# The first product of one MLP by seven block products in place of eight, in a two-layer fp32 transformer kernel on one core

## The chip, the core and the metric

The kernel runs on one core of one Trainium2 chip. The metric is the device time of one execution in microseconds. A core has TensorE (PE, matrix products into the eight banks of PSUM), VectorE (DVE), ScalarE (ACT), GpSimd (POOL) and SyncE (SP), which issues the DMAs. Each engine works through its own instructions in order.

## The reference

Two layers over 512 latent and 256 context tokens of 1024 features, all in fp32. Layer 0 mixes by neighbourhood attention, layer 1 by sliding-window attention; each mixer is followed by an MLP with 4096 hidden features. Cut to what matters here (layer 0, both token streams):

```python
h_lat = h_lat + ga1 * (mixer(u_lat) @ wo);  h_ctx = h_ctx + cga1 * (mixer(u_ctx) @ wo)
u = modulate(rms_norm(h, g_mlp), shift, scale)      # h * (1 + scale) + shift
h = h + ga2 * (jnp.square(jax.nn.relu(u @ w1)) @ w2)   # w1: 1024 x 4096, w2: 4096 x 1024
```

Shifts, scales and gates come from `ada_w`, 1024 x 6144 for each layer, times a conditioning vector for the latent and one for the context tokens ("ada").

## The kernel before

Features lie on the 128 partitions: `hT` has eight tiles of 128 features (`KT = 8`), with the 512 latent and the 256 context tokens (`L`, `C`, `T = 768`) in the free dimension. To keep fp32 precision every operand is split in two parts of type fp32r, x = H + L (`split`: a copy on ScalarE rounds to H, a subtraction on GpSimd or VectorE gives L), and a product is three matmuls: wH·uH + wH·uL + wL·uH.

The order of work isn't that of the source. `_build` records steps (engine, operands) in a `Plan`; `Plan.search` then runs a list scheduler with costs of its own over them, many times with shaken ranks, keeps the best order found up to each `mark()`, and writes each engine's queue in that order. Steps made with `gv` may go to GpSimd or VectorE, with `sv` to ScalarE or VectorE, as the planner finds best; `squared` to ScalarE or VectorE.

**Wo.** After attention, `Wo` makes eight feature tiles `f` for the latent tokens (24 matmuls of 512 columns each) and eight for the context tokens (24 of 256). Its weights come in two halves of four units (each one DMA of 128 x 1024 and one split): `take(0)` covers f = 0..3 and puts the first unit into `wx`, the others into `wslots[2]`, `[0]`, `[3]`; `early` starts three tiles while the last head pair's attention runs; `rest` does what is left, adds to `hT` with VectorE, and `Stats` sums the squares.

**The MLP of layer 0** (`mlp(0, True, ...)`). u is made by `modulate`: for each f a multiply-add on VectorE, an activation on ScalarE for uH, another multiply-add for uL. Then come 16 chunks of 256 hidden features (two blocks j of 128). `mlp1` makes the first product of a chunk: for each j and each of the eight k three matmuls for 512 latent columns and three for 256 context columns, 96 in all; `relu2` takes the square of the relu and splits it into `hH`, `hL` (a ring of four). `mlp2` makes the second product: for each of the eight f six matmuls of 512 and six of 256 columns, and after each group VectorE adds the scaled sum to `hT`:

```python
v.scalar_tensor_tensor(out=h, in0=ps, scalar=mods[layer][:, 5, f, col : col + 1], in1=h, op0=ALU.mult, op1=ALU.add)
```

The first product uses PSUM banks 4 and 5 (latent), 0 and 1 (context), the second 2 and 3 (latent), 6 and 7 (context). The weights of w1 and w2 come through `Stream`, four units of 128 x 1024 ahead, into eight slots. Between the products the generator `ada` for layer 1 runs piece by piece: for each of 6 kinds and 8 k a 128 x 1024 tile of `ada_w` is multiplied by two columns of the conditioning vector (ScalarE, or GpSimd for one of them where k is odd) and added into two accumulators (VectorE or GpSimd).

**Layer 1's start.** `kv1` normalizes the latent tokens (`modulate` reads `hT`), stores `hT` to `h_d`, and projects keys and values; `roped` multiplies them by tables in `rope`. Mask and `rope` lie in the columns of `FA` that held the context part of `hT`; they are filled before `kv1` (GpSimd memset and select, a DMA of `rope`, four GpSimd products).

Of the kernel before, what the change touches and what calls it, by code (L numbers as in the profile page):

```python
# [11 lines left out]
F32 = mybir.dt.float32  # L12
R32 = mybir.dt.float32r
# [538 lines left out]

LAST = 3
# [7 lines left out]
def _build(nc, tc, a, es):  # L561
# [145 lines left out]
    hT_lat = FA[:, 0:4096].rearrange("p (f n) -> p f n", f=KT)  # L707
    hT_ctx = FA[:, 4096:6144].rearrange("p (f n) -> p f n", f=KT)
# [8 lines left out]
    def mm(ps, st, mv, start, stop):  # L717
        pe.matmul(ps, st, mv, start=start, stop=stop)
# [17 lines left out]
    def ada(layer, kinds, ring, acc, tmp, ps, depth):  # L736
# [3 lines left out]
        jobs = [(kind, k) for kind in kinds for k in range(KT)]  # L740
        w = {}

        def fetch(i):
            if i < len(jobs):
                kind, k = jobs[i]
                w[i] = ring.next(1024)
                load(w[i], a["ada_w"][layer, k * 128 : (k + 1) * 128, kind * D : (kind + 1) * D])
# [12 lines left out]
        for i in range(depth):  # L760
            fetch(i)
        for i, (kind, k) in enumerate(jobs):
            x = w.pop(i)
            if k == 0:
                (g.tensor_scalar(out=acc[0], in0=x, scalar1=s32[:, k, 0:1], scalar2=None, op0=ALU.mult) if k % 2 else s.activation(acc[0], x, AF.Copy, scale=s32[:, k, 0:1]))
                s.activation(acc[1], x, AF.Copy, scale=s32[:, k, 1:2])
            else:
                (g.tensor_scalar(out=tmp, in0=x, scalar1=s32[:, k, 0:1], scalar2=None, op0=ALU.mult) if k % 2 else s.activation(tmp, x, AF.Copy, scale=s32[:, k, 0:1]))
                gv.tensor_tensor(out=acc[0], in0=acc[0], in1=tmp, op=ALU.add)
                s.activation(x, x, AF.Copy, scale=s32[:, k, 1:2])  # L770
                gv.tensor_tensor(out=acc[1], in0=acc[1], in1=x, op=ALU.add)
            if k < KT - 1:
                fetch(i + depth)
                yield
# [5 lines left out]
            row = x[:, 0:512]  # L780
            s.copy(row, ps)
            yield
            finish(kind, row)
            fetch(i + depth)
# [53 lines left out]
    class Stream:  # L838
# [14 lines left out]
        def next(self, fill=True):  # L853
            self.fill(1)
            u = self.items[self.i][1]
            self.i += 1
            if fill:
                self.fill(self.ahead)
            return u[:, 0:1024], u[:, 1024:2048]

# [369 lines left out]

    class Wo:
# [86 lines left out]
    wo0 = Wo(0, True, lambda ctx, f: (hT_ctx if ctx else hT_lat)[:, f])  # L1318
# [99 lines left out]
    ad = ada_pe(0, (2, 3, 4, 5), Ring(FA, 2048, 1024, 2), lambda kind: banks[5], 2)  # L1418
# [12 lines left out]
    wo0.take(0, Stream(Ring(FA, FX, 1024, 2), [(a["wo0"][0, q], u) for q, u in enumerate((wx, wslots[2], wslots[0], wslots[3]))], 4))  # L1431
# [11 lines left out]
    def mlp(layer, T_ctx, stream, tmp, side, st_lat, st_ctx, between=None, after_ctx=None):  # L1443
        if T_ctx:
            p1, p1c, p2, p2c = Banks(4, 5), Banks(0, 1), Banks(2, 3), Banks(6, 7)
        else:
            p1, p1c, p2, p2c = Banks(4, 5, 0, 1), Banks(0), Banks(2, 3, 6, 7), None
        nt = T if T_ctx else L
        hr = Ring(RA, RW + 14336, 1536, 4)
        def relu2(ps, n, hH, hL):  # L1450
# [7 lines left out]
        def mlp1(c, between=None):  # L1458
# [3 lines left out]
            def start(j, fill=True):  # L1462
                W[j] = stream.next(fill)
                u = hr.next()
                hs.append((u[:, 0:nt], u[:, 768 : 768 + nt]))

            def part(pss, js, uH, uL, hook=None, lo=0):
                hi = lo + pss[0].shape[1]
                for k in range(KT):
                    if hook and k == 4:  # L1470
                        hook()
                    sl = slice(k * 128, k * 128 + 128)
                    for ps, j in zip(pss, js):
                        wH, wL = W[j]
                        mm(ps, wH[:, sl], uH[:, k, lo:hi], k == 0, False)
                        mm(ps, wH[:, sl], uL[:, k, lo:hi], False, False)
                        mm(ps, wL[:, sl], uH[:, k, lo:hi], False, k == KT - 1)

            def lat(*js, hook=None, halves=False):
                pss = [p1.next() for j in js]  # L1480
                if halves:
                    for j in js:
                        part([pss[j][:, 0:256]], [j], uH_lat, uL_lat)
                        if j == 0:
                            hook()
                    part([ps[:, 256:512] for ps in pss], js, uH_lat, uL_lat, lo=256)
                else:
                    part(pss, js, uH_lat, uL_lat, hook)
                for ps, j in zip(pss, js):
                    relu2(ps, 512, hs[j][0][:, 0:512], hs[j][1][:, 0:512])  # L1490

            def ctx(*js):
                if T_ctx:
                    pss = [p1c.next()[:, 0:256] for j in js]
                    part(pss, js, uH_ctx, uL_ctx)
                    for ps, j in zip(pss, js):
                        relu2(ps, 256, hs[j][0][:, 512:768], hs[j][1][:, 512:768])

            if between:
# [3 lines left out]
                if T_ctx:  # L1503
                    lat(0, 1, hook=between)
                else:
                    lat(0, 1, hook=between, halves=True)
                stream.fill(stream.ahead)
                ctx(0, 1)
            else:
                start(0)  # L1510
                lat(0)
                run(side, 1)
                ctx(0)
                run(side, 1)
                start(1)
                lat(1)
                run(side, 1)
                ctx(1)
                run(side, 1)
            return hs  # L1520

        def mlp2(c, hs, last):
            W = [stream.next() for j in range(2)]

            def one(ps, f, lo, hi, hT, col):
                at = col * 512
# [7 lines left out]
                h = hT[:, f, lo - at : hi - at]  # L1534
                v.scalar_tensor_tensor(out=h, in0=ps, scalar=mods[layer][:, 5, f, col : col + 1], in1=h, op0=ALU.mult, op1=ALU.add)

            if last and T_ctx:
                pc = Banks(1, 6, 0)
                for f in range(KT):
                    one(pc.next()[:, 0:256], f, 512, 768, hT_ctx, 1)  # L1540
                    st_ctx.step(hT_ctx[:, f], v if f == KT - 1 else g)
                pl = Banks(2, 3, 4, 5)
                for f in range(KT):
                    one(pl.next(), f, 0, 512, hT_lat, 0)
                    st_lat.step(hT_lat[:, f], v if f == KT - 1 else g)
                    if f == 1:
                        st_ctx.finish()
                        after_ctx()
            elif last:
                for f in range(KT):  # L1550
                    n = 512 if f < KT - 1 else 256
                    for lo in range(0, 512, n):
                        one(p2.next()[:, 0:n], f, lo, lo + n, hT_lat, 0)
                        sy.dma_start(a["out"][:, f, lo : lo + n], hT_lat[:, f, lo : lo + n])
            else:
                for f in range(KT):
                    one(p2.next(), f, 0, 512, hT_lat, 0)
                    if T_ctx:
                        one(p2c.next()[:, 0:256], f, 512, 768, hT_ctx, 1)
# [3 lines left out]
        p1c = Banks(0)  # L1563
        for c in range(NCH):
            now = nxt
            if c == NCH // 2 and T_ctx:
                mark()
            if c + 1 < NCH:
                nxt = mlp1(c + 1)
                if T_ctx or c:  # L1570
                    stream.eng = v
            if c == NCH - 2 and T_ctx:
                run(side)
                p2, p2c = Banks(2, 3, 4, 5), Banks(6, 0, 1)
            mlp2(c, now, c == NCH - 1)

    def mlp_items(layer):

        w1, w2 = ([(a[n][layer, 2 * c], a[n][layer, 2 * c + 1]) for c in range(16)] for n in ("w1", "w2"))
# [10 lines left out]
    def load1(gr):  # L1590
# [3 lines left out]
    RX, RY = region((R32, 2048), (F32, 2048))  # L1594
    wslots.append(RX[:])
    wu = Slots(*(wslots[i] for i in (4, 5, 6, 7, 0, 1, 2, 3)))
    stream = Stream(
        Ring(FA, FX, 1024, 3),
        [(a["wo0"][1, q], wu.next()) for q in range(4)] + [(x, wu.next()) for x in mlp_items(0)]
        + [(a["wkv1"][q], wslots[q]) for q in range(4)] + [(a["wq1"][0, q], wq[q]) for q in range(2)],  # L1600
        4)
    adar = Ring(FA, FX + 3072, 1024, 2)
    tmp = Ring(FA, FX + 5120, 512, 5)
    tmp2 = Ring(FA, FX + 3072, 512, 9)
    Rm = fr(7680, 768)
    R_lat, R_ctx = Rm[:, 0:512], Rm[:, 512:768]
    st = (Stats(R_lat, 512, tmp2, banks[2]), Stats(R_ctx, 256, tmp2, banks[3]))
# [403 lines left out]
```

## Time and profile before

| | |
|---|---|
| median of 3 runs | 1602.92 us (1602.74 to 1604.47) |
| profiled execution | 1604.45 us, of which the span of the profile is 1602.7 us |
| granted TensorE clock, mean | 0.997 |
| busy: PE / DVE / ACT / POOL | 1581.8 / 1116.0 / 761.0 / 235.6 us |
| second products of the first MLP, first add to the last chunk's first add | 496.3 to 985.1 us |
| DMA | 171.17 MB, mean 107 GB/s |

How to read the rows. A row of groups gives engine, operation, tiles out<-in (without buffer numbers: `pq` are PSUM banks, `RA` the fp32r arrays, `FA` the fp32 arrays, `RX`/`RY` appear as `R`), shape, count, then busy time in us, mean ns of one, and the idle time of the engine before them with what ended it. A row of the timeline or of the chain gives start, us, engine and what, with neighbouring instructions of like tiles merged under the shape of the first. A row of a stretch gives its length, then for PE, PEld (weight loads), DVE, ACT and POOL the busy time and the count, then granted clock, DMA share and GB/s. All instructions bear one line number, that of the place where the planned order is written out (L547), so groups are told apart by their tiles and shapes.

### The profile page before, as it was taken

What the parts mean: (1) busy time and instruction counts of PE and PEld (TensorE: products, weight loads), DVE (VectorE), ACT (ScalarE), POOL (GpSimd) and SP (SyncE); (2) the same over time, 40 slices, a digit from 0 to 9 for tenths busy, and PEclk for the clock granted to TensorE, in tenths of its full rate; (3) what the DMA queues carried; (4) which work ended last, traced back from release to release, by engine and by line L of the source; (5) the groups of instructions that cost most, each with busy time, mean ns of one, the idle gap of its engine ahead of it and who ended that gap; (6) DMA issues with size and microseconds to landing.
All of it is one profiled execution on the core that took longest, in us unless ns stands there. A gap on an engine that the chain in (4) does not pass through costs nothing.

```text
span 1602.7 us, 24512 instructions
## 1 busy us (share of the span) xinstructions
PE 1581.8 (99%) x9372; PEld 1336.8 (83%) x9372; DVE 1116.0 (70%) x2193; ACT 761.0 (47%) x1554; POOL 235.6 (15%) x197
## 2 busy tenths in 40 slices
PE   7999999999999999999999999999999999999999
PEld 5888888987888888888888888798877888888887
DVE  4887765676479667677686857898885855556564
ACT  4676665676355233435343423677782523323320
POOL 0101001010013122313141300232100000000000
PEclk9999999999999999999999999999999999999999
DMA  9654443224314233433342321101044323223211
GB/s 348 173 162 121 124 138 108 61 73 143 104 66 159 91 110 115 132 106 119 122 142 93 119 80 66 33 28 59 29 122 162 106 88 98 89 84 116 93 40 53
DMA packets 60309, 171.17 MB, mean 107 GB/s; under 512 B 7296, under 2 KB 17056, under 8 KB 60064
## 3 DMA queue, kind: packets, MB, share of 16 engines
q1 hardware_dynamic: 60192, 169.61, 33.1%
q8 instruction: 73, 1.20, 0.3%
q14 instruction: 44, 0.36, 0.1%
HBM read 165.30 MB, written 7.43 MB: 108 GB/s over the span
## 4 chain that ended last, share of the span: by engine, by line
PE 91%; DVE 4%; DMA 2%; ACT 1%; issue 1%; SPq 0%; POOL 0%; DVEq 0%; ACTq 0%; POOLq 0%
PE pq L547 91%; DVE RA L547 2%; DVE FA L547 1%; DMA R<-inv_d 1%; DMA FA<-in_ada_w_dram 1%; ACT RA L547 0%; ACT FA L547 0%; DMA FA<-in_wqkv_dram 0%; DVE R L547 0%; DMA FA<-in_xT_dram 0%; SPq L547 0%; DVE smalls L547 0%; ACT R L547 0%; DMA FA<-h_d 0%; POOL FA L547 0%
## 5 line engine op out<-in xcount | busy, mean ns | idle before, releaser
L547 PE MATMUL pq<-RA 128*128 128x512 f32 (+3 forms) x6560 | 1282.8, 348 | 5.2 <-DVE RA L547 2.2
L547 PEld LDWEIGHTS pq<-RA 128*128 128x128 f32 x6560 | 1053.6, 189 | 154.8 <-issue 10.5
L547 ACT CAST RA<-FA 128x1024 fp32r<-128x1024 f32 (+3 forms) x283 | 223.8, 811 | 377.9 <-PE pq L547 273.2
L547 DVE SCALAR_TENSOR_TENSOR FA<-pq,mods,FA 128x512 f32<-128x512 f32 (+1 forms) x413 | 261.7, 659 | 166.2 <-PE pq L547 165.0
L547 DVE TENSOR_TENSOR RA<-FA,RA 128x1024 fp32r<-128x1024 f32 (+3 forms) x236 | 242.6, 1038 | 94.2 <-ACT RA L547 89.6
L547 PE MATMUL pq<-RA,R 128*128 128x512 f32 (+1 forms) x870 | 189.9, 351 | 0.1
L547 PEld LDWEIGHTS pq<-RA,R 128*128 128x128 f32 x870 | 145.3, 189 | 24.2 <-issue 0.8
L547 POOL TENSOR_TENSOR RA<-FA,RA 128x512 fp32r<-128x512 f32 (+2 forms) x47 | 77.0, 1639 | 502.0 <-ACT RA L547 461.4
L547 PE MATMUL pq<-ident,FA 128*128 128x128 f32 x800 | 133.2, 274 | 0.9 <-DVE RA L547 0.3
L547 DVE TENSOR_TENSOR R<-R,FA 128x1024 f32<-128x1024 f32 x84 | 109.6, 1331 | 15.0 <-ACT FA L547 8.6
L547 PEld LDWEIGHTS pq<-ident,FA 128*128 128x128 f32 x800 | 96.7, 140 | 17.3 <-issue 2.0
L547 ACT ACTIVATE FA<-FA,smalls 128x512 f32<-128x512 f32 (+1 forms) x120 | 89.0, 742 | 43.3 <-DVE smalls L547 42.6
L547 POOL TENSOR_SCALAR FA<-FA,s 128x1024 f32<-128x1024 f32 x24 | 75.3, 3136 | 197.6 <-DMA FA<-in_ada_w_dram 115.7
L547 ACT ACTIVATE FA<-pq 128x512 f32<-128x512 f32 (+1 forms) x96 | 49.8, 522 | 102.9 <-PE pq L547 99.7
L547 ACT ACTIVATE FA<-FA,s 128x1024 f32<-128x1024 f32 x60 | 69.0, 1151 | 53.7 <-POOL FA L547 43.1
L547 POOL TENSOR_TENSOR FA<-FA 128x256 f32<-128x256 f32 (+2 forms) x51 | 40.5, 800 | 281.4 <-ACT FA L547 143.5
L547 DVE SCALAR_TENSOR_TENSOR FA<-pq,FA 128x512 f32<-128x512 f32 (+1 forms) x96 | 56.7, 595 | 35.9 <-ACT FA L547 35.8
L547 ACT ACTIVATE FA<-FA 128x256 f32<-128x256 f32 (+1 forms) x130 | 58.1, 454 | 47.8 <-DVE FA L547 39.7
L547 POOL TENSOR_TENSOR FA<-FA,smalls 128x128 f32<-128x128 f32 (+2 forms) x54 | 34.5, 640 | 299.7 <-DVE smalls L547 212.3
L547 ACT COPY R<-pq 128x512 f32<-128x512 f32 (+4 forms) x133 | 62.5, 486 | 20.2 <-PE pq L547 19.2
L547 PE MATMUL pq<-R 128*64 128x256 f32 (+3 forms) x432 | 68.4, 456 | 1.9 <-DVE FA L547 1.9
L547 DVE SCALAR_TENSOR_TENSOR RA<-pq,cst,RA 64x128 fp32r<-64x128 f32 (+2 forms) x152 | 57.9, 383 | 14.2 <-ACT RA L547 11.6
(88 smaller groups left out, 912.6 us busy)
## 6 DMA issues: line engine op xcount, KB each, us to landing
FA<-in_w_dram SPq DMA_DIRECT2D x128, 512.0 KB
FA<-in_ada_w_dram SPq DMA_DIRECT2D x80, 512.0 KB
FA<-in_wqkv_dram SPq DMA_DIRECT2D x24, 384.0 KB
FA<-in_wo_dram SPq DMA_DIRECT2D x16, 512.0 KB
FA<-in_ada_dram SPq DMA_DIRECT2D x10, 512.0 KB
FA<-in_wq_dram SPq DMA_DIRECT2D x8, 512.0 KB
R<-inv_d SPq DMA_DIRECT2D x16, 208.0 KB
R<-in_ada_dram SPq DMA_DIRECT2D x6, 512.0 KB
```

Of the source, the lines that this page charges most:

```text
L547: tc.keep_in_program_order(getattr(e, f)(*map(real, args), **{k: real(x) for k, x in kw.items()}))
```

## The change

1. `mlp` is divided: `mlp_one` (layer 1) is what it was, `mlp_zero` (layer 0) is new. The first product is seen as blocks: u is 2 x 2 blocks (k in two halves of `KH = 4` tiles, tokens in two halves of `HT = 384`), a chunk's weights are 2 x 2 blocks too (k halves, j). Chunk 0 (`plain`) makes the eight block products. Chunks 1 to 15 make seven (`head` two, `tail` five), each 4 x 3 matmuls of 384 columns, on sums of weight blocks and of u blocks.
2. The sums of u are made once (`u_first`, `u_rest`, `u_last`), in place in `hT`; so `Wo0` stores h to `hs_d` (16 DMAs) and `u_last` loads it back (8 DMAs). The sums of weights are made for every chunk: four `gv` additions and seven splits of 512 columns, and four splits of w2 quarters (`w20`).
3. In the second product, f = 0, 1, 2 of the latent tokens stay in banks 2, 3, 6 over all chunks; the rest shares banks 5 and 7. The first product uses 4, 0, 1.
4. `ada` works on halves of 512 columns: for k = 0 two ScalarE activations, else two VectorE multiply-adds into the accumulators, with no GpSimd.
5. `Wo0` takes its weights by column quarters: two units (k = 0..3, k = 4..7) serve two f. The order of slots is 2, 0, 3, wx for f = 0..3, and 2, 0, 3, 1 for f = 4..7. `lat_done` (making u) is called before the context tiles f = 4..7.
6. `hT` is one array of 768 columns per f, so mask and `rope` are filled in `kv1` after the stores to `h_d` (`tables`).

```diff
-    def ada(layer, kinds, ring, acc, tmp, ps, depth):
+    def ada(layer, kinds, ring, acc, ps):
...
+            for r in range(2):
+                o = acc[r][:, h * 512 : h * 512 + 512]
+                if k == 0:
+                    s.activation(o, x, AF.Copy, scale=s32[:, k, r : r + 1])
+                else:
+                    v.scalar_tensor_tensor(out=o, in0=x, scalar=s32[:, k, r : r + 1], in1=o, op0=ALU.mult, op1=ALU.add)
...
+    class Wo0:
...
+        def one(self, bk, f, ctx, st):
...
+            v.scalar_tensor_tensor(out=h, in0=ps, scalar=mods[0][:, 2, f, ctx : ctx + 1], in1=h, op0=ALU.mult, op1=ALU.add)
+            st.step(h, v if f == KT - 1 and not ctx else g)
+            sy.dma_start(hs_d[:, f, L:T] if ctx else hs_d[:, f, 0:L], h)
...
+    first = Stream(Ring(FA, FX, 1024, 2), [(a["wo0"][q], u) for q, u in enumerate((wslots[2], wslots[0], wslots[3], wx))], 4)
...
+    def u_of(lo, hi, R, ctx):
+        for f in (0, 4, 1, 5, 2, 6, 3, 7):
+            h = hT[:, f, lo:hi]
+            v.scalar_tensor_tensor(out=h, in0=h, scalar=amod[0][:, 1, f, ctx : ctx + 1], in1=R, op0=ALU.mult, op1=ALU.mult)
+            s.activation(h, h, AF.Identity, bias=mods[0][:, 3, f, ctx : ctx + 1])
+    def u_first():
+        u_of(0, L, R_lat, 0)
+        for f in range(KT):
+            blocks(f, 0, "11" if f < KH else "21")
+    def u_rest(ring):
+        u_of(L, T, R_ctx, 1)
+        for k in range(KH):
+            blocks(k, 1, "12")
+            blocks(k + KH, 1, "22")
+        for k in range(KH):
+            b11, b12, b21, b22 = (hT[:, f, at : at + HT] for f in (k, k + KH) for at in (0, HT))
+            t2 = ring.next(HT)
+            to = lambda name: [x[:, k] for x in UC[name]]
+            v.tensor_tensor(out=b11, in0=b12, in1=b11, op=ALU.subtract)
+            v.tensor_tensor(out=t2, in0=b22, in1=b11, op=ALU.subtract)
+            split(*to("t2"), t2)
+            split(*to("t1"), b11)
+            v.tensor_tensor(out=b12, in0=b22, in1=b12, op=ALU.subtract)
+            split(*to("t3"), b12)
+            v.tensor_tensor(out=b21, in0=b21, in1=t2, op=ALU.subtract)
+    def u_last():
+        for k in range(KH):
+            blocks(k + KH, 0, "t4")
+        for f in range(KT):
+            sy.dma_start(hT[:, f], hs_d[:, f])
+    def mlp_zero(queue, xs, side, st_lat, st_ctx, between, after_ctx):
+        p1, p2 = Banks(4, 0, 1), Banks(5, 7)
+        held = {0: banks[2], 1: banks[3], 2: banks[6]}
...
+            def head(self):
+                self.a, b = self.bk.next()[:, 0:HT], self.bk.next()[:, 0:HT]
+                product(self.a, "11", True, last=False)
+                x = self.kept(self.a)          # sv copy of the bank
+                product(b, "21", True)
+                self.added(0, 0, b, x)         # v add, relu, square, split
...
+            def tail(self):
+                a_, c_ = self.a, self.bk.next()[:, 0:HT]
+                product(a_, "t2", False, last=False)
+                y = self.kept(a_)
+                product(c_, "t1", True, last=False)
+                z = self.kept(c_)
+                product(a_, "t3", False, last=False)
+                self.added(1, 1, a_, z)
+                product(c_, "22", False)
+                self.added(0, 1, c_, y)
+                product(a_, "t4", False)
...
+        pairs = [Pair(Banks(4, 5)), Pair(Banks(0, 1, 2))]
+        queue.ahead = 3
+        W = [queue.next(False) for i in range(4)]
+        pairs[0].plain(W, 0)
+        between()                              # u_rest
+        pairs[1].head()
+        pairs[0].plain(W, 1)
+        queue.ahead = AHEAD                    # 5
+        u_last()
+        pairs[1].tail()
+        for c in range(NCH):
...
+            if 0 < c < NCH - 1:
+                x = Pair()
+                x.head()
+                run(side, 2)
+                x.tail()
+                run(side, 2)
+                pairs.append(x)
...
+            second(pairs[c].h, c == 0, c == NCH - 1)
...
-    g.memset(mask, 0.0)
...
+    def tables():
+        g.memset(mask, 0.0)
...
         for f in range(KT):
             sy.dma_start(h_d[:, f], hT_lat[:, f])
+        tables()
```

More of the change, by code (lines that the diff above doesn't have):

```diff
@@ L859, in next, with __init__, fill @@
             return u[:, 0:1024], u[:, 1024:2048]
+    class Queue:
+        def __init__(self, items, ahead):
+            self.items, self.ahead, self.got, self.i = items, ahead, [], 0
+        def fill(self, n):
+            while len(self.got) < min(self.i + n, len(self.items)):
+                self.got.append(self.items[len(self.got)]())
+        def next(self, fill=True):
+            self.fill(1)
+            u = self.got[self.i]
+            self.i += 1
+            if fill:
+                self.fill(self.ahead)
+            return u
     def run(gen, n=None):
@@ L1439, in _build @@
     split_o(7)
[L1443 to L1448, printed above, removed]
+    HT = T // 2
+    KH = KT // 2
+    UB = dict(zip(("11", "21", "22", "t2", "t1", "t3", "t4", "12"), (0, 6144, 3072, 9216, 12288, 15360, 18432, 18432)))
+    UC = {n: [RA[:, o + i * 1536 : o + i * 1536 + 1536].rearrange("p (k n) -> p k n", k=KH) for i in range(2)] for n, o in UB.items()}
@@ L1474, in part, with out @@
                         wH, wL = W[j]
[L1475 to L1497, printed above, removed]
+                        mm(ps, wH[:, sl], uH_lat[:, k, lo:hi], k == 0, False)
+                        mm(ps, wH[:, sl], uL_lat[:, k, lo:hi], False, False)
+                        mm(ps, wL[:, sl], uH_lat[:, k, lo:hi], False, k == KT - 1)
+            def out(ps, j):
+                relu2(ps, L, *hs[j])
             if between:
@@ L1502, in mlp1 @@
                 start(1, False)
[L1503 to L1506, printed above, removed]
+                pss = [p1.next() for j in range(2)]
+                for j in range(2):
+                    part([pss[j][:, 0:256]], [j])
+                    if j == 0:
+                        between()
+                part([ps[:, 256:512] for ps in pss], (0, 1), lo=256)
+                for j in range(2):
+                    out(pss[j], j)
                 stream.fill(stream.ahead)
-                ctx(0, 1)
             else:
[L1510 to L1519, printed above, removed]
+                for j in range(2):
+                    start(j)
+                    ps = p1.next()
+                    part([ps], [j])
+                    out(ps, j)
             return hs
@@ L1533, in one @@
                     mm(ps, wL[:, sl], hH[:, lo:hi], False, j == 1)
[L1534 to L1559, printed above, removed]
@@ new lines, in one @@
+                h = hT_lat[:, f, lo:hi]
+                v.scalar_tensor_tensor(out=h, in0=ps, scalar=mods[1][:, 5, f, 0:1], in1=h, op0=ALU.mult, op1=ALU.add)
+            for f in range(KT):
+                if not last:
+                    one(p2.next(), f, 0, 512)
+                    continue
+                n = 512 if f < KT - 1 else 256
+                for lo in range(0, 512, n):
+                    one(p2.next()[:, 0:n], f, lo, lo + n)
+                    sy.dma_start(a["out"][:, f, lo : lo + n], hT_lat[:, f, lo : lo + n])
@@ new lines, in operand, with first_items, at, made @@
+    def operand(x):
+        u = ops.next()
+        split(u[:, 0:512], u[:, 512:1024], x)
+        return u[:, 0:512], u[:, 512:1024]
+    def first_items(n):
+        w, t = {}, {}
+        def at(i, h):
+            if i not in w:
+                w[i] = raw.next()
+                sy.dma_start(w[i], a["w1"][0, 2 * n + i])
+            return w[i][:, h * 512 : h * 512 + 512]
+        def made(name, x, y, op):
+            t[name] = sums.next()
+            gv.tensor_tensor(out=t[name], in0=x, in1=y, op=op)
+            return t[name]
+        def s2():
+            made(1, at(1, 0), at(1, 1), ALU.add)
+            return operand(made(2, t[1], at(0, 0), ALU.subtract))
+        if n == 0:
+            return [lambda i=i: operand(at(i // 2, i % 2)) for i in range(4)], []
+        return ([lambda: operand(at(0, 0)), lambda: operand(at(0, 1))],
+                [s2, lambda: operand(t[1]), lambda: operand(made(3, at(0, 0), at(1, 0), ALU.subtract)),
+                 lambda: operand(made(4, at(0, 1), t[2], ALU.subtract)), lambda: operand(at(1, 1))])
```

269 lines of the change are left out of this document (200 added, 69 removed).

## The prediction

> **What bounds the kernel now.** First the page's head, its busy times and the chain that ended last: a PE that is busy all the time can still be waiting inside, so the chain has to say the same.
>
> ```profile
> span 1602.7 us, 24512 instructions
> PE 1581.8 (99%) x9372; PEld 1336.8 (83%) x9372; DVE 1116.0 (70%) x2193; ACT 761.0 (47%) x1554; POOL 235.6 (15%) x197
> PE 91%; DVE 4%; DMA 2%; ACT 1%; issue 1%; SPq 0%; POOL 0%; DVEq 0%; ACTq 0%; POOLq 0%
> ```
>
> Then the chain in order of time, and the busy times by stretch, for the stage that is changed: from the end of Wo's products (455 us) to the end of the first MLP (1003 us).
>
> ```profile
> 587.92 424.09 PE pq L547 x2433
> ...
> 496.30:985.10 488.80, 488.66 (x2815) 423.60 (x2814) 348.75 (x472) 182.89 (x240) 110.33 (x49) 1.00 0.34 108
> ```
>
> The first row is one unbroken run of matmuls, 424.09 / 2433 = 174.3 ns apart. The second gives, after the stretch's length, the busy times of PE, PEld, DVE, ACT and POOL, then the clock and the DMA share. TensorE has 0.14 us free in 488.8, at full clock, with DVE at 71%. A matmul taken away here shortens the kernel by its spacing, as long as nothing else fills the place.
>
> **The saving.** Per 256 hidden columns the first product is now 96 matmuls, 48 of 512 and 48 of 256 columns. After, seven block products of 4 x 3 matmuls of 384 columns make 84. The spacings, from the timeline of PE (start, time from the first start to the last end, first form, count; a run's last matmul ends its own duration after its start):
>
> ```profile
> 455.81 4.96 PE L547 MATMUL pq<-RA 128*128 128x512 f32 x21
> 451.49 1.72 PE L547 MATMUL pq<-RA 128*128 128x256 f32 x13
> 355.23 2.41 PE L547 MATMUL pq<-RA 128*128 128x384 f32 x13
> ...
> L547 PE MATMUL pq<-RA 128*128 128x512 f32 x3272 | 844.9, 396 | 3.3 <-DVE smalls L547 1.7 <-DVE RA L547 0.9 <-ACT RA L547 0.5
> L547 PE MATMUL pq<-RA 128*128 128x256 f32 x2360 | 355.4, 286 | 1.9 <-DVE RA L547 1.3 <-DVE FA L547 0.4
> L547 PE MATMUL pq<-RA 128*128 128x384 f32 x864 | 175.4, 344 | 0.0
> ```
>
> (4.96 - 0.396) / 20 = 228 ns, (1.72 - 0.286) / 12 = 119.5 ns, (2.41 - 0.344) / 12 = 172 ns. Now 48 x (228 + 119.5) = 16.68 us; after, 84 x 172 = 14.45 us, 2.2 us less. By the long run's mean, 12 x 174.3 = 2.1 us. I take 2.1: 15 of the 16 chunks change, so **-31.5 us** (32.5 to 33 by the single rows). Chunk 0 stays at eight block products, 96 x 172 ns = 16.5 us: nothing.
>
> **What VectorE gets instead, per chunk.** The rows of before that carry prices:
>
> ```profile
> L547 DVE TENSOR_TENSOR R<-R,FA 128x1024 f32<-128x1024 f32 x79 | 102.0, 1318 | 13.9 <-ACT FA L547 7.8 <-POOL FA L547 5.7
> L547 DVE SCALAR_TENSOR_TENSOR FA<-pq,mods,FA 128x512 f32<-128x512 f32 x119 | 87.5, 745 | 41.7 <-PE pq L547 41.4
> L547 DVE SCALAR_TENSOR_TENSOR FA<-pq,mods,FA 128x256 f32<-128x256 f32 x117 | 54.6, 478 | 23.4 <-PE pq L547 22.9
> L547 DVE TENSOR_TENSOR RA<-FA,RA 128x512 fp32r<-128x512 f32 x15 | 10.3, 689 | 7.6 <-ACT RA L547 7.6
> L547 DVE TENSOR_TENSOR RA<-FA,RA 128x256 fp32r<-128x256 f32 x14 | 6.5, 463 | 2.8 <-ACT RA L547 2.8
> ...
> L547 POOL TENSOR_SCALAR FA<-FA,s 128x1024 f32<-128x1024 f32 x22 | 68.2, 3098 | 182.2 <-DMA FA<-in_ada_w_dram 115.7 <-ACT RA L547 35.8 <-DVE FA L547 20.6
> L547 POOL TENSOR_TENSOR RA<-FA,RA 128x512 fp32r<-128x512 f32 x13 | 23.6, 1817 | 95.5 <-ACT RA L547 81.9 <-DVE R L547 8.1 <-issue 5.6
> ...
> 449.26 3.40 DVE L547 SCALAR_TENSOR_TENSOR FA<-FA,amod 128x512 f32<-128x512 f32 x5 [1.32 <-ACT FA L547]
> ```
>
> Removed: three of eight 512-wide adds into h (their sums stay in PSUM), relu2's two products, the 1024-wide splits, ada's 1024-wide additions. Left or added: 5 x 0.745 + 8 x 0.478 = 7.5 us of adds from PSUM; ada by VectorE alone, 42 x 4 multiply-adds of 512 over 14 chunks, 12 x 0.68 (the last row: 3.40 / 5) = 8.2 us; 3 additions of block products at 0.58 (between the 256 and 512 rows) = 1.7 us; eleven weight splits, four weight sums and four 384-wide splits, which POOL may take too, 15 x 0.69 + 4 x 0.58 = 12.7 us. All on VectorE this is 30.1 us of a 31.3 us chunk (96 second-product matmuls and 84 first at 174 ns); with six of them on POOL (6 x 1.82 = 10.9 us there, and the 68.2 us of TENSOR_SCALAR leave POOL) 26.0 us, 83%. It was 348.75 / 14.5 = 24.1 us of 33.7. So it fits, tighter than before. In-order queues at 83 to 96% will be late now and then: **+2 us**, from 0 to 15 x 0.7 = 10 (chunks as long as 32.0 us). ScalarE loses ada's multiplications and gets some 20 small copies; at 182.89 of 488.8 busy it costs nothing.
>
> **The start of the MLP.** Today u is made by two multiply-adds and one activation per feature tile. After, it is made in place, split in blocks of 384, and combined by 16 subtractions and 12 more splits before the five products of the first pair's tail can run. What covers it:
>
> ```profile
> 436.00:443.70 7.70, 7.70 (x37) 6.37 (x36) 1.26 (x2) 0.63 (x1) 0.00 (x0) 1.00 0.01 2
> 443.70:455.20 11.50, 11.50 (x93) 11.02 (x92) 8.90 (x14) 7.53 (x12) 0.00 (x0) 1.00 0.01 1
> 455.20:486.00 30.80, 30.59 (x172) 26.53 (x171) 27.20 (x45) 19.56 (x36) 7.19 (x4) 1.00 0.39 128
> ```
>
> TensorE's work from the last latent Wo product (443.7) to the end of that tail: context Wo 11.5, four blocks of chunk 0 8.3, head 4.2, the other four 8.3, tail 10.4: 42.7 us. VectorE's in the same time: 4.3 of Wo's adds and squares, 8 x 0.68 + 8 x 0.42 = 8.8 to make u, 32 block splits and 16 subtractions at 0.58 = 27.8, weights 2 splits and 1 sum (the first nine operands fit their slots earlier, when VectorE is idle) plus 4 of w2 = 4.8, outputs 11 x 0.58 = 6.4: 52 us, of which POOL can take splits worth about 9 us in 20 us of its own. So 43 against 42.7, behind a wait of about 5 us until the mean square is known (449.26 is the first multiply-add, row above). The block t2 for k = 3 comes last, and PE can fill only with what is independent: products of the held sums of chunk 0, whose weights are then also queued on VectorE. I take **+4 us**; 0 if POOL and the fill do it, 52 - 42.7 + 3 = 12 if POOL helps nowhere.
>
> A long hole costs twice, as an earlier stage shows: one microsecond of waits, then a lower clock (column before the DMA share).
>
> ```profile
> 360.00:370.00 10.00, 9.10 (x57) 7.55 (x56) 9.11 (x28) 9.61 (x30) 1.26 (x2) 1.00 0.42 130
> 370.00:380.00 10.00, 9.01 (x49) 5.10 (x50) 6.26 (x12) 3.69 (x8) 0.00 (x0) 0.83 0.72 221
> 470.00:480.00 10.00, 10.00 (x60) 8.84 (x60) 8.18 (x12) 4.04 (x7) 4.26 (x1) 1.00 0.76 260
> ```
>
> (0.83 over 10 us is 1.7 us of work.) The Trainium skill ("TensorE: Matmul & The Clock Gate", Part 1) says that an idle window of about 3.4 us halves the clock for the next such window; by that a hole at the start would add an estimated 1.7 us, and the 0.83 agrees with it in size.
>
> DMA: 16 stores of h to hs_d on SP at 413 to 456 us (the queue is idle, shares 0.01 above) and 8 reloads of 3.1 MB in all at about 480, where 260 GB/s already move; 12 us at that rate. Behind them on SP stand weights; the first reader is chunk 0's context add, after the 10.4 us tail. **+1 us**, 0 to 5.
>
> **The two PSUM banks of the second product.** Sums that are not held share banks 5 and 7; today there are four. Latent tile f + 1 needs the bank of tile f, with only six 256-wide matmuls between (0.72 us). From Wo, such an eviction:
>
> ```profile
> 442.21 1.52 PE L547 MATMUL pq<-RA,R 128*128 128x512 f32 x6
> 443.57 2.20 PE L547 MATMUL pq<-RA 128*128 128x256 f32 x17
> 443.77 0.75 DVE L547 SCALAR_TENSOR_TENSOR FA<-pq,mods,FA 128x512 f32<-128x512 f32 x1 [3.10 <-PE pq L547]
> ```
>
> PE goes on at 443.57, the eviction ends at 444.52: 0.95 us, 0.23 more than the cover; five times a chunk 1.2 us, times 15 17 us, if PE had nothing else. It has: the next pair's products use other banks (4, 0, 1), and the planner's order mixes them in. I take **+1 us**, 0 to 17.
>
> **Wo by quarters.** The unit wx, free early, is filled first today; after, it is fourth. Its matmuls (k = 0, 1 for three tiles: 18 x 0.228 = 4.1 us) fill holes around 363 us, before the next weights are cast:
>
> ```profile
> 367.24 1.66 ACT L547 CAST RA<-FA 128x1024 fp32r<-128x1024 f32 x3
> 370.99 1.63 PE L547 MATMUL pq<-RA 128*128 128x256 f32 x6 [1.30 <-DVE RA L547]
> ```
>
> After, the first quarter can be cast as soon as its slot is free and brings 24 matmuls at once. **+1 us**, -1 to +4. f = 4 and 5 must wait for f = 0 and 1, latent and context; between lie context tiles 2 and 3, 48 x 0.12 = 5.8 us, over one cast and split: nothing, at worst 2 us.
>
> **Mask and rope, moved.** They lie in columns of h now, so they wait until modulate has read them and h_d has them; the DMA of rope moves on SP behind the eight h_d stores, and POOL's four products behind that.
>
> ```profile
> 1007.67 0.33 SPq L547 DMA_DIRECT2D FA<-in_rope_dram  x1
> 1011.02 0.74 POOL L547 TENSOR_TENSOR FA<-FA,gsw 128x256 f32<-128x256 f32 x1 [7.39 <-DMA FA<-in_rope_dram]
> 1027.31 0.74 DVE L547 SCALAR_TENSOR_TENSOR FA<-FA,amod 128x512 f32<-128x512 f32 x1
> 1033.36 0.42 DVE L547 TENSOR_TENSOR FA<-FA 128x256 f32<-128x256 f32 x1
> ```
>
> The last modulate read ends at 1028.05; 3.35 us for the DMA as today and three products of 0.74 make 1033.6, against the first use at about 1033.4. **+1 us**, 0 to 4 (VectorE waits in order behind it, while PE has three key tiles of 2.7 us to go on with).
>
> **Sum.** -31.5 + 2 + 4 + 1 + 1 + 1 + 1 = -21.5. The profiled execution took 1604.45 us (span 1602.7), 1.5 over the median of 1602.92; 1604.45 - 21.5 = 1583.0, or 1581.4 on the median's footing. I say 1581.
>
> **Rivals.**
> 1. *Everything is covered.* The extra terms vanish but for about 3 us: 1602.92 - 31.5 + 3 = 1574. For it: 0.14 us idle today, and queues ordered ahead of time. Against: the start has no slack by my count. 0.22.
> 2. *VectorE becomes the bound.* Where POOL runs beside it, an operation with two SBUF inputs is slowed:
>
> ```profile
> 456.96 3.09 POOL L547 TENSOR_TENSOR FA<-FA 128x256 f32<-128x256 f32 x3 [35.50 <-issue]
> 457.07 3.53 DVE L547 SCALAR_TENSOR_TENSOR FA<-FA,amod 128x512 f32<-128x512 f32 x3
> ```
>
> 3.53 / 3 = 1.18 us against 0.68. Such operations are 8.2 + 12.7 us of the chunk; a third of them slowed so adds up to 5 us, to 31 us if POOL takes six, and with 5% of waits 32.6: 15 x 1.3 = 20 us. 1581 + 18 = 1599; no gain at all from 33.4 us a chunk. Against it: ada can slide between chunks. 0.13. The Trainium skill ("GPSIMD Engine Reference", 1. Specifications) says GpSimd shares its SBUF interfaces with VectorE and contends with instructions of two SBUF inputs; the two rows agree, at 1.7 times.
> 3. *Slower: the two banks stall PE.* If the eviction also queues behind another VectorE operation (0.7 us each), the wait is 0.23 + 0.7, five times a chunk, 15 chunks: 70 us; PE's fill is limited, as a later pair's outputs need the h slots of the present one. From 2.1 us a chunk it eats the gain; at half the 70 us the time is 1581 + 34 = 1615. Against: finely mixed orders of 512 and 256 in today's stage leave PE no hole. 0.09.
> 4. *Seven products do not save*, since 384-wide matmuls with a wait between blocks take 0.2 us each: 84 x 0.2 = 16.8 us a chunk, as much as now, and the other terms of 10 us stay: 1602.92 + 10 = 1613. The 384 row speaks against. 0.02.
>
> **Numbers.** The forecast's own case, 1577 to 1590, has 0.54. With rivals 1 and 2 the range is 1572 to 1598. A measurement here tells 0.2% (3.2 us) from no change. Faster: 0.54 + 0.22 + two thirds of 0.13 = 0.85; the same: 0.05, the rest of rival 2 and the near side of 3; slower 0.10.
>
> **What would show it.** Right: 384-wide matmuls about 172 ns apart in the MLP, 15 x 12 fewer; the stretch from chunk 0's second product to the last about 30 us shorter with PE still over 99%; VectorE at 80 to 90% there. PE's idle time at the first tail, waiting for VectorE (RA), sizes the +4; PE waiting on FA from the second product's adds sizes the banks. Wrong: PE under 97% in the MLP's middle, waits on VectorE in every chunk, or a lower clock there.

## The result and the profile after

The changed kernel takes 1574.93 us (median of 4 runs, 1574.79 to 1575.73), against 1602.83 us for the kernel before on the same chip: ratio 0.983, 95% interval 0.9813 to 0.9847. That is 27.9 us faster and inside the range, but 6 us under the forecast of 1581 and below the forecast's own case (1577 to 1590). It is the figure of rival 1 (1574), in which all that was added is covered. The page's head and chain, then the chain in order of time:

```profile
span 1574.0 us, 24810 instructions
PE 1551.8 (99%) x9192; PEld 1339.5 (85%) x9192; DVE 1178.4 (75%) x2412; ACT 792.9 (50%) x1749; POOL 179.4 (11%) x182
PE 93%; DVE 3%; DMA 2%; ACT 1%; issue 0%; SPq 0%; POOL 0%; DVEq 0%; ACTq 0%
...
468.91 333.49 PE pq L547 x1902
803.07 1.35 DVE R L547 x2
809.01 171.79 PE pq L547 x974
```

Matmuls fall by exactly 180 = 15 x 12 (9372 to 9192), PE's busy time by 30.0 us; PE's idle time in the whole span grows by 1.3 us only, from 20.9 to 22.2. Together this is the 28.7 us by which the span fell. TensorE is still the chain. Its spacing in the two unbroken stretches of the chain is 175.3 and 176.4 ns (174.3 before).

To see where the 28.7 us come from, the two spans are cut at the same places: the last product of layer 0's attention, the last of Wo's adds, the second product's first and last add, layer 1's first attention product, Wo1's first add. The rows of stretches (length, then busy PE, PEld, DVE, ACT, POOL, clock, DMA): the start of the MLP, the chunk stage, kv1 and the last stage, first of before, then of after:

```profile
456.00:496.33 40.33, 40.12 (x228) 34.99 (x228) 36.46 (x50) 26.58 (x45) 14.25 (x8) 1.00 0.43 144
496.33:1003.66 507.33, 507.19 (x2922) 440.03 (x2922) 365.70 (x503) 192.60 (x259) 115.25 (x56) 1.00 0.35 109
1003.66:1080.68 77.02, 75.32 (x467) 65.44 (x465) 72.28 (x185) 54.34 (x124) 25.64 (x34) 1.00 0.08 25
1218.02:1602.70 384.68, 380.38 (x1811) 318.17 (x1809) 227.64 (x300) 113.36 (x159) 22.06 (x12) 1.00 0.28 91
```

```profile
456.50:495.16 38.66, 38.50 (x219) 37.18 (x218) 35.66 (x72) 35.19 (x78) 4.33 (x4) 1.00 0.39 121
495.16:971.33 476.17, 475.50 (x2731) 433.11 (x2730) 419.10 (x688) 209.34 (x397) 70.81 (x48) 1.00 0.41 126
971.33:1050.34 79.01, 75.24 (x460) 65.78 (x458) 72.63 (x187) 54.34 (x120) 24.80 (x31) 0.98 0.09 31
1185.71:1574.00 388.29, 381.84 (x1816) 321.55 (x1814) 231.72 (x302) 115.20 (x159) 17.41 (x10) 1.00 0.27 90
```

| stage, us | before | after | difference | matmuls | PE's idle time |
|---|---|---|---|---|---|
| up to the last product of attention 0 | 403.8 | 401.1 | -2.7 | +1 | -1.4 |
| to the last of Wo's adds | 52.2 | 55.4 | +3.2 | +21 | 0.0 |
| to the second product's first add (start) | 40.3 | 38.7 | -1.7 | -10 | 0.0 |
| chunk stage | 507.3 | 476.2 | **-31.2** | -192 | +0.5 |
| kv1 | 77.0 | 79.0 | +2.0 | -7 | +2.1 |
| attention 1 | 137.3 | 135.4 | -2.0 | +1 | -1.9 |
| from Wo1's first add to the end | 384.7 | 388.3 | +3.6 | +6 | +2.1 |

The last two columns are differences too; a matmul is counted in the stage in which it starts. The saving stands in the chunk stage, where PE is idle for 0.7 of 476.2 us although VectorE went from 72% to 88% busy. The planner also moves matmuls over the cuts: the chunk stage lost 12 more than the 180 that were left out, an estimated 2.1 us of its 31.2 at 174 ns each, and Wo's stage got 21 more. So a stage's length alone doesn't price an edit; its matmuls and PE's idle time have to be read with it. Outside the chunk stage, what is lost and what is won nearly cancel (+2.4 in all). The last stage became longer without one line of its source being changed: in it PE waits 2.48 us for GpSimd, up to 1221.6 us, and the granted clock is then 0.50 for 3.4 us.

### The profile page after: what moved, and what is told of

The parts are those of the page before. It is cut to its first block, busy times and chain, and to the rows that moved or that the text cites. A ratio compares the mean times of both kernels' runs of the same rounds, so it can differ in the third digit from the quotient of the medians.

```text
span 1574.0 us, 24810 instructions
## 1 busy us (share of the span) xinstructions
PE 1551.8 (99%) x9192; PEld 1339.5 (85%) x9192; DVE 1178.4 (75%) x2412; ACT 792.9 (50%) x1749; POOL 179.4 (11%) x182
## 4 chain that ended last, share of the span: by engine, by line
PE 93%; DVE 3%; DMA 2%; ACT 1%; issue 0%; SPq 0%; POOL 0%; DVEq 0%; ACTq 0%
PE pq L547 93%; DVE RA L547 1%; DVE FA L547 1%; ACT RA L547 1%; DMA R<-inv_d 0%; DMA FA<-in_ada_w_dram 0%; ACT FA L547 0%; DMA FA<-in_wo_dram 0%; SPq L547 0%; DMA FA<-in_xT_dram 0%; POOL FA L547 0%; DVE R L547 0%; DVE smalls L547 0%; DMA FA<-in_cT_dram 0%; ACT R L547 0%
## 5 line engine op out<-in xcount | busy, mean ns | idle before, releaser
L547 PE MATMUL pq<-RA 128*128 128x512 f32 (+2 forms) x5492 | 1097.7, 351 | 4.0 <-ACT RA L547 1.9
L547 PEld LDWEIGHTS pq<-RA 128*128 128x128 f32 x5492 | 908.1, 190 | 113.9 <-issue 7.6
L547 ACT CAST RA<-FA 128x512 fp32r<-128x512 f32 (+4 forms) x353 | 239.1, 697 | 283.6 <-PE pq L547 205.6
L547 PE MATMUL pq<-RA,R 128*128 128x512 f32 (+2 forms) x1758 | 349.6, 344 | 0.2 <-DVE RA L547 0.2
L547 PEld LDWEIGHTS pq<-RA,R 128*128 128x128 f32 x1758 | 294.4, 188 | 32.1 <-ACT R L547 1.7
L547 DVE TENSOR_TENSOR RA<-FA,RA 128x512 fp32r<-128x512 f32 (+4 forms) x319 | 257.9, 827 | 76.9 <-ACT RA L547 75.6
L547 ACT ACTIVATE FA<-FA 128x384 f32<-128x384 f32 (+2 forms) x216 | 103.1, 483 | 69.3 <-DVE FA L547 61.0
L547 DVE SCALAR_TENSOR_TENSOR R<-R,s 128x512 f32<-128x512 f32 x168 | 135.2, 842 | 0.0
L547 DVE TENSOR_TENSOR FA<-FA 128x512 f32<-128x512 f32 (+3 forms) x139 | 79.5, 584 | 9.8 <-ACT FA L547 7.0
L547 DVE TENSOR_TENSOR R<-FA,R 128x512 fp32r<-128x512 f32 (+1 forms) x79 | 65.9, 840 | 26.7 <-ACT R L547 24.9
L547 PE MATMUL pq<-R 128*64 128x256 f32 (+3 forms) x432 | 67.2, 450 | 0.0
```

The costliest lines, as they stand in the source:

```text
L547: tc.keep_in_program_order(getattr(e, f)(*map(real, args), **{k: real(x) for k, x in kw.items()}))
```

## The experiments

Two theories at first. *A: the gain is the matmuls left out, and the planner's free order hides everything that was added.* *B: the gain is partly that of the other edits (sums held in PSUM, ada, Wo), and hidden waits eat a part of it.* Runs without an interval are single runs; the kernel before took 1601.99 to 1602.98 us beside them. Every edit also gives the planner another problem, and so another order, which by itself moves the whole time by some 5 us (*another seed*, below). So the single runs are read by the chunk stage, which hardly moves with the order, and not by a few microseconds of the whole.

**Eight products again.**

```diff
     def u_last():
-        for k in range(KH):
-            blocks(k + KH, 0, "t4")
...
-                x.head()
+                W = [queue.next() for i in range(4)]
+                x.plain(W, 0)
...
-                x.tail()
+                x.plain(W, 1)
...
-        if n == 0:
+        if n >= 0:
             return [lambda i=i: operand(at(i // 2, i % 2)) for i in range(4)], []
```

> The changed kernel with the seven block products undone and nothing else: all 16 chunks make eight block products of 384 columns, with no sums of weights; the sums of u are still computed, but not used. Theory A (the gain is the 15 x 12 matmuls of 384 columns that are left out, at about 174 ns): 31 us more than the changed kernel, 1574.9 + 31 = 1606, within 0.3% of the kernel before. Theory B (part of the gain comes from what came with it: sums held in PSUM, the other ada, Wo by quarters): well under 1603, for instance 1590 if half of it does. Theory C (seven products cost hidden waits on VectorE that eight would not): under 1600.

Measured: 1604.89 us, ratio to the kernel before 1.0014 (1.0005 to 1.0024). Its chunk stage:

```profile
489.00:1000.90 511.90, 510.50 (x2930) 467.09 (x2929) 346.96 (x555) 180.67 (x330) 41.69 (x29) 1.00 0.38 118
```

The whole is 30.0 us longer than the changed kernel, with 180 matmuls more. The chunk stage is 35.7 us longer, with 199 matmul records more: besides the 180, some of other stages. VectorE has less to do in it (347 for 419 us). All edits but the seven products are together worth nothing that can be told from the order's chance; theory A.

**Nothing held in PSUM.**

```diff
-        p1, p2 = Banks(4, 0, 1), Banks(5, 7)
-        held = {0: banks[2], 1: banks[3], 2: banks[6]}
+        p1, p2 = Banks(4, 0, 1), Banks(2, 3, 6, 5, 7)
+        held = {}
```

> The changed kernel without sums held in PSUM over the chunks: all eight latent tiles are added to h in every chunk, and the second product takes banks 2, 3, 6, 5, 7 in turn. It gives VectorE 3 x 0.745 = 2.2 us more a chunk, on a stage where it is busy 419.1 of 476.2 us. Theory A (VectorE has room until it is near 100%): about 450 of 477 us busy, no more than 3 us longer. Theory B (in-order VectorE at 88% is already the edge): the 2.2 us come through, 15 x 2.2 = 33 us at most, 10 or more to be seen.

Measured: 1573.58 us, no longer than the changed kernel.

```profile
492.53:972.66 480.13, 479.39 (x2753) 438.11 (x2752) 452.14 (x726) 213.34 (x407) 84.18 (x60) 1.00 0.40 125
```

The stage is 4 us longer with 22 matmul records more. VectorE is busy 452.14 of 480.13 us (94%), and PE is idle for 0.7 us, as in the changed kernel. Theory A; the held sums save VectorE work that it had time for.

**One bank.**

```diff
-        p1, p2 = Banks(4, 0, 1), Banks(5, 7)
+        p1, p2 = Banks(4, 0, 1), Banks(5)
```

> The changed kernel with one PSUM bank instead of two for the sums of the second product that are not held. Each of 13 sums a chunk must be added to h (0.75 or 0.48 us, and some 0.2 to get there) before the next can start. Theory A (TensorE fills such waits with products of the next pair): a few us, under 10. Theory B (the fill is nearly used up, since the next pair can run ahead by little): 13 waits of 0.7 to 0.95 us, some 10 us a chunk, up to 150 us.

Measured: 1579.22 us, 4.3 us more. Its chunk stage, and what PE and its weight loads wait for there:

```profile
494.40:977.20 482.80, 479.55 (x2745) 434.48 (x2744) 424.38 (x682) 209.87 (x397) 81.43 (x56) 1.00 0.41 125
PEld pq L547 <- DVE FA L547: 9.0, 11, 1.4
```

(A row of waits gives the total in us, their number and the longest.) Eleven waits of weight loads for VectorE's adds in 15 chunks of 13 sums: nearly every one is filled, and PE is idle for 3.3 us in the stage (0.7 with two banks). Theory A.

**TensorE in the source's order.** Each matmul step of the chunk loop is made to depend on the one before it in the source:

```diff
+        if step.eng == "PE":
+            if self.inorder and self.lastpe is not None:
+                d.add(self.lastpe)
+            self.lastpe = i
```

> The changed kernel with TensorE's work in the chunk loop (from chunk 0's second product to the last chunk) tied to the order of the source, so that nothing can be put into a wait; the other engines are planned as before. Theory A (mixing the next pair's products into the second product is what hides the two banks): TensorE waits 0.23 to 0.9 us five times a chunk, 17 to 70 us longer, with waits on FA seen in the second product. Theory B (the two banks suffice by themselves): under 5 us longer.

Measured: 1611.05 us, 36 us more, slower than before the change. The chunk stage, and PE's waits in it:

```profile
490.20:1008.60 518.40, 499.62 (x2792) 447.15 (x2791) 450.33 (x744) 206.93 (x386) 44.76 (x30) 1.00 0.38 116
PEld pq L552 <- DVE FA L552: 25.1, 50, 1.3
PE pq L552 <- DVE FA L552: 10.8, 21, 1.1
```

The two rows, 35.9 us together, overlap: a wait can be seen twice, at a weight load and at its matmul (27.4 us of the stage are covered by either). PE is idle for 18.8 us. That isn't the whole loss, since the time of a matmul (282 ns for 256 columns) is longer than its spacing (120 ns) and hides the first part of a wait. Counted by the starts of the matmuls, against the median spacing of each width in the stage, TensorE loses 40.5 us here and 9.8 in the changed kernel; most of it is at the 256-column matmuls, on average 151 ns apart. Theory A: 36 us in all, in the middle of its 17 to 70, with the waits on FA.

**The same order with five banks.** The edits of the last and of *nothing held* together.

> The kernel of e4_in_order (TensorE in source order through the chunk loop) with no sums held and five banks in turn for the second product, as in e2_nothing_held. Theory A (the 36 us that the source order cost are waits for the two banks): most of them go, 1573.6 to 1585, and TensorE's waits for VectorE's adds (FA) fall from 36 us in the loop to under 10. Theory B (they are waits for the first product's additions and squares, or for weights): 1600 or more again.

Measured: 1579.95 us.

```profile
491.90:977.20 485.30, 481.90 (x2780) 441.88 (x2779) 452.48 (x744) 214.49 (x405) 67.88 (x47) 1.00 0.40 124
PEld pq L552 <- DVE FA L552: 0.9, 2, 0.7
PE pq L552 <- DVE FA L552: 0.4, 1, 0.4
```

33.1 of the 42.2 us that the chunk stage had become longer are gone, although VectorE has 256 sums to add in it for 211. PE is idle for 3.4 us, and the loss by the starts is back at 10.5 us. So the source order's cost was the two banks, and either more banks or the mixed order avoids it.

**More work for VectorE.**

```diff
+            for _ in range(5):
+                v.scalar_tensor_tensor(out=pad_, in0=pad_, scalar=s32[:, 0, 0:1], in1=pad_, op0=ALU.mult, op1=ALU.min)
```

> The changed kernel with ten more VectorE multiply-adds of 320 columns (some 0.48 us each, on columns used for nothing else) in each of 14 chunks, 67 us of work in all, on a stage of 476 us where VectorE is busy 419. Theory A (VectorE was no bound, but is next): 419 + 67 = 486 us do not fit in 476; 10 to 20 us longer, VectorE over 97% busy, TensorE waiting for it. Theory B (VectorE's busy time contains waits for its shared port and for in-order turns, so that it can't reach 97%): 30 us longer or more.

Measured: 1578.32 us, 3.4 us more.

```profile
492.70:977.00 484.30, 484.08 (x2780) 442.81 (x2780) 468.01 (x802) 219.38 (x419) 75.96 (x53) 1.00 0.40 127
```

The function is called twice in each of 14 chunks. Both theories expected more. Of the 140 operations 115 stand in this stage (67.2 us of busy time), the others before it. VectorE's busy time is 49 us longer than in the changed kernel and stands at 97%; PE still doesn't wait (0.2 us). The stage is 8 us longer, but with 49 matmul records more, so it took in work of other stages. Neither theory is right: 97% is reached without a loss in this stage. Just before it, between Wo's last add and the second product's first, PE is idle for 3.1 us (0.2 in the changed kernel); no run shows whether the operations put there are the cause.

**The start in the source's order.** The edit of *TensorE in the source's order*, from the rest of Wo to the end of the first tail.

> The changed kernel with TensorE's work tied to the order of the source from the rest of Wo to the end of the first pair's tail, so that nothing of chunk 0's second product or of later pairs can fill the waits for the blocks of u. Theory A (the start was covered only because the planner mixed other products in): 4 to 12 us longer, as the prediction's count without fill, with TensorE waiting for RA near the tail. Theory B (VectorE and ScalarE make the blocks in time by themselves): under 2 us longer.

Measured: 1586.14 us, 11.2 us more, as A said, but not where A said. The PE rows with a wait in brackets, then the stretch after the first of them and the whole of Wo's stage:

```profile
400.65 6.21 PE L552 MATMUL pq<-RA 128*128 128x512 f32 x13 [2.71 <-ACT RA L552]
...
447.10 1.38 PE L552 MATMUL pq<-FA,ones 128*128 128x512 f32 x2 [2.29 <-DVE FA L552]
477.61 7.03 PE L552 MATMUL pq<-RA,R 128*128 128x384 f32 x37 [0.19 <-DVE RA L552]
```

```profile
401.40:406.40 5.00, 5.00 (x13) 3.94 (x13) 2.71 (x4) 1.68 (x3) 0.51 (x1) 0.50 0.54 184
...
397.60:461.30 63.70, 58.69 (x329) 51.15 (x326) 38.73 (x60) 27.77 (x48) 7.26 (x6) 0.92 0.32 112
```

Wo's stage is 63.7 us long for 55.4. The holes are at the start of Wo's rest (2.7 us, and then half the clock for some 6 us) and before the mean square's matmul (2.3 us). The stage behind it is 6.7 us longer, but with 25 matmul records more. At the tail, where the blocks of u are wanted, VectorE makes PE wait 0.2 us, even without any fill. Theory B holds for the blocks; the cost is that of older waits which the free order hid.

**Without the tables.**

```diff
     def tables():
+        return
```

> The changed kernel without the mask and the rope tables of layer 1 (memset, selects, rope's DMA and its four products are left out; layer 1 computes with what lies in those columns). Theory A (their move behind modulate's reads of h costs TensorE the 3.6 us hole in kv1): the stage from the last add of the first MLP to layer 1's first attention product falls from 79.0 us to 77 or less, and the hole goes. Theory B (the hole is VectorE's, which makes u with 1.2 us a multiply-add, and would be there anyway): 79 us and a hole of 2 us or more stay.

Layer 1 then computes with whatever lies in the columns of mask and `rope`. Measured: 1572.91 us. kv1's stage stays:

```profile
968.90:1048.70 79.80, 77.36 (x467) 66.57 (x465) 73.32 (x192) 54.46 (x123) 21.55 (x27) 0.98 0.08 28
```

79.8 us for 79.0. PE's idle time in it goes from 3.8 to 2.4 us, of which one hole is 2.0, and VectorE is at 92% either way. Theory B: stage and hole stay. But this is one order, and those of the eleven other traces with the change have 2.9 to 5.9 us of idle time in this stage, so that the tables cause a part of it is neither shown nor excluded.

**Another seed of the search**, for the changed kernel and for the one before, and twice the tries:

```diff
-        rnd, pe = random.Random(1), self.ALL.index("PE")
+        rnd, pe = random.Random(2), self.ALL.index("PE")
```

> The changed kernel with another seed of the planner's random search, and nothing else. It tells how far a stage's time moves with the order alone. Theory A (the 3.6 us that layer 1's last stage, from Wo1's first add on, got longer without a change in its source are the search's chance): that stage anywhere between 383 and 389 us, the whole within 4 us of 1574.9. Theory B (something in the change made that stage longer): 388 us again.

> The kernel of e8_seed again (the changed kernel, another seed), timed against the kernel before. Theory A (its 5.5 us under the changed kernel are a better order found by chance, and stay): 1569 to 1571, ratio 0.979 to 0.981, and kv1's stage near 76 us again. Theory B (they are one run's chance): 1573 to 1576.

> The kernel before with that same other seed. It tells whether the change's gain depends on the seed. Theory A (the search's chance moves either kernel by some 5 us, and the change is worth 31 us less what other stages lose): 1597 to 1608. Theory B (the kernel before was only unlucky in its seed, and a good part of the 27.9 us is chance): 1590 or less.

> The changed kernel with twice the planner's tries (32 for 16). Theory A (what the kernel still loses outside the MLP, 2 to 6 us, is the search's): 1568 to 1574. Theory B (the planner's own costs, not its search, decide what waits on the chip, so a better plan is no better there): 1573 to 1578.

Measured: e8 1569.37 us in one run; e9, the same kernel in four runs, 1570.86 us, ratio 0.9797 (0.9783 to 0.981); e10 1595.48 us, ratio 0.9953 (0.994 to 0.9965); e11 1571.13 us, ratio 0.9793 (0.9776 to 0.9811). The chunk stages of the two seeds of after and before (e8, e10):

```profile
494.80:969.10 474.30, 474.30 (x2727) 432.69 (x2726) 421.39 (x681) 209.45 (x400) 81.54 (x56) 1.00 0.40 125
494.40:1001.70 507.30, 507.30 (x2926) 440.66 (x2925) 367.16 (x512) 193.34 (x260) 98.70 (x48) 1.00 0.35 110
```

507.3 and 507.3 before, 476.2 and 474.3 after: this stage hardly knows the seed. The others do: the last stage, whose source the change leaves alone, took 380.9 to 388.3 us in the twelve traces with the change, kv1 76.2 to 85.5. E9 and e11 come out at their A. E8 leaves its question open: the last stage took 387.3 us, which suits both theories, and the whole is 5.6 us under the changed kernel, more than A allowed. E10 lies 1.5 us below its A and 5.5 above its B: by the ratio, the kernel before had an order 7.5 us worse than another seed gives, and with that same seed the change is worth 1595.48 - 1570.86 = 24.6 us, ratio 0.985. So of the 27.9 us some 3 are the order's chance, as far as two seeds can tell. E9 and e11 are faster than the changed kernel by a new order, nothing more.

## Why the prediction was right

In short: the saving was placed and sized rightly, and the costs, 10 us in the sum, were mostly too big. PE's busy time fell by 30.0 us where 31.5 was forecast, and its idle time grew by 1.3. The time lies in the range because the saving is right; the case that came true is rival 1, to which the forecast gave 0.22, and its ground against it, that the start has no slack, was wrong.

- *The saving, -31.5.* Right by the number of matmuls exactly (180), by PE's busy time to 1.5 us (30.0), and in the stage where it was placed. That the stage's difference agrees to 0.3 us (-31.2) is partly luck, as 12 more matmuls left it by the order. (By the single rows the working gives 15 x 2.23 = 33.4, a little above the 32.5 to 33 written there.) *Eight products again* shows that it is the whole gain.
- *VectorE per chunk, +2.* The term was too big: with the banks' it cost about 0.5 us (PE idle 0.14 us before, 0.7 after). The size of VectorE's load was too small, 419.1 / 14.5 = 28.9 us a chunk where 26.0 was forecast: POOL took 45 of the additions and splits, three a chunk and not six, and ada's multiply-adds took longer than 0.68. The groups of the chunk stage:

```profile
L547 DVE SCALAR_TENSOR_TENSOR R<-R,s 128x512 f32<-128x512 f32 x168 | 135.2, 842 | 0.0
...
L547 POOL TENSOR_TENSOR R<-FA,R 128x512 fp32r<-128x512 f32 x15 | 24.2, 1618 | 132.1 <-ACT R L547 92.4 <-DVE RA L547 39.7
```

  135.2 / 168 = 0.80 us each. The trace tells why: the 134 of these multiply-adds that no GpSimd instruction overlaps take 0.74 to 0.75 us, the 34 that one overlaps 1.23 on average and up to 1.79. That 88% would bring late turns was the wrong step: 94% and 97% brought none that PE felt.
- *The start, +4.* This is the term that was mis-sized, and it carries most of the difference to the measured time. It came to nothing: PE was idle 0.2 of the 38.7 us from Wo's last add to the second product's first. (That the stage became 1.7 us shorter is its 10 matmuls fewer.) The rows answering to those of before:

```profile
443.30:454.50 11.20, 11.20 (x86) 10.72 (x85) 9.03 (x15) 9.10 (x17) 1.36 (x1) 1.00 0.04 13
454.50:486.40 31.90, 31.74 (x179) 30.63 (x178) 29.56 (x60) 28.73 (x66) 4.92 (x4) 1.00 0.21 55
...
478.04 0.51 PE L547 MATMUL pq<-RA,R 128*128 128x512 f32 x2
478.38 0.51 PE L547 MATMUL pq<-RA 128*128 128x384 f32 x2
478.73 2.84 PE L547 MATMUL pq<-RA,R 128*128 128x256 f32 x16
481.41 0.34 PE L547 MATMUL pq<-RA 128*128 128x384 f32 x1
481.58 1.55 PE L547 MATMUL pq<-RA,R 128*128 128x512 f32 x6
482.97 0.51 PE L547 MATMUL pq<-RA 128*128 128x384 f32 x2
```

  VectorE did 38.6 us up to 486.4, not 43. Matmuls of 256 and 512 columns, chunk 0's second product, stand between the tail's last 384-wide ones, which the forecast named as the only fill; they are few (14 from 478.0 to 484.1, an estimated 2.8 us by the spacings). The in-order start shows that the blocks were nearly in time even without it.
- *Two banks, +1.* The size is not told apart from the 0.5 us above; the condition was the right one: without the mixing the banks cost 36 us, near half of rival 3's 70. Rival 3 was a true mechanism that the planner's order switches off.
- *hs_d's stores and reloads, +1.* No wait of PE on them.
- *Wo by quarters, +1.* Attention ends 2.7 us earlier and Wo 0.5 later: within its -1 to +4. Wo's stage has 21 matmuls more. Which part is the order of the units and which the search's chance was not told apart.
- *Mask and rope, +1.* kv1 became 2.0 us longer with 7 matmuls fewer, and PE has a hole there, after which the granted clock is 0.50 for 3.4 us:

```profile
999.91 0.86 PE L547 MATMUL pq<-ident,FA 128*128 128x128 f32 x4 [3.40 <-DVE FA L547]
```

  Without the tables the stage is as long, with a hole of 2.0 us; with another seed and the tables it is 76.2. But PE's idle time in kv1 is 2.4 to 5.9 us in all twelve traces with the change and 1.7 and 1.5 in the two of the kernel before, so something in the change, and not only the order, costs TensorE time here. What it is stays open: the size lies in the 0 to 4 of the forecast, the mechanism is not shown.
- *Rival 2 (VectorE as the bound)* is refuted as far as 97%; the slowing beside POOL is there (0.75 to 1.23 us, above) but is paid from VectorE's idle time. *Rival 4* is refuted by the spacing: 2731 matmul records in 476.17 us, 174.4 ns each.
- Not foreseen: the search's chance, some 5 us for the changed kernel and 7.5 for the kernel before, which no term of the sum had. The last stage's +3.6 us is of that kind. The wait of over 2 us for GpSimd with half the clock behind it, which stands in the changed kernel, is in three of the twelve traces with the change (the changed kernel, e4, e8), and there the last stage takes 387.3 to 388.3 us; in the other nine it takes 380.9 to 386.3.

## What to carry to other kernels

Where one engine is the chain for a whole stage and is idle for less than 1% of it, expect its saved work to come through nearly in full; here it did while an engine beside it went to 88%, and that engine could go to 97%, its work being done ahead of time. Scarce buffers, here two PSUM banks, cost next to nothing if the bound engine's queue has other work mixed in, and here 36 us if it has not; so price the order together with the buffers. Where a search makes the order, build the kernel with another seed before a difference of a few microseconds is given a cause, and count the instructions of a stage before its length is compared.

## What the runs showed of the hardware

- In *the start in the source's order*, after a hole of 2.7 us in PE's work, the granted clock was 0.50 over the next 5 us (13 matmuls of 512 columns instead of 22): a hole well under the 3.4 us window that the Trainium skill ("TensorE: Matmul & The Clock Gate", Part 1) gives is enough here. In the kernel before, the 1.30 us hole at 370 us, which the prediction shows, was enough: 0.50 from 371.6 us for 3.4 us. The length of the hole alone doesn't decide. E8 and e9 are the same kernel with the same two holes: behind that in kv1 (2.59 and 2.58 us) the clock stayed at 1.00 in e8 and fell to 0.50 for 3.4 us in e9, behind that in the last stage (2.22 and 2.21 us) it was the other way round.
- VectorE was busy for 97% of a 484 us stage while PE was idle for 0.2 us of it.
- The eight multiply-adds that make uL in kv1, from a first operand read in rows (a strided view), took 1.2 us each for 512 columns, in the kernel before too (1.1 to 1.25 without GpSimd beside them), against 0.74 for the plain ones of the MLP before. They add an estimated 4 us to VectorE's 72.6 in that stage. That the view is the reason is not shown by a run:

```profile
987.48 2.43 DVE L547 SCALAR_TENSOR_TENSOR RA<-FA,mods,RA 128x512 fp32r<-128x512 f32 x2 [0.22 <-ACT RA L547]
```
